# PE operands at one address modulo 256, scores grouped by form, and the u/z stage begun within v's last steps

## The chip, the cores and the metric

The kernel runs on one core of one Trainium2 chip. The metric is the time of one execution on the device in microseconds (us); smaller is better. The core's engines run side by side, each with its own queue of instructions that it works through in order: PE (TensorE, matmuls; its weight loads are listed apart as PEld), DVE (VectorE), ACT (ScalarE), POOL (GpSimd) and SP (SyncE, which here issues DMAs). They wait for one another by semaphores.

## The reference

One gMLP layer, then one sliding-window attention layer, on x of 1024 tokens by 1024 channels, all in float32:

```python
u, v, z = split(rms_norm(x) @ w_in, 3)          # 2048 channels each
u = gelu(u); v = layer_norm(gelu(v))
s = causal(w_s) applied to v in chunks of 128 tokens, per group of 256 channels, + b_s
h = x + rms_norm((u * s * silu(z)) @ w_out)
k, v = rms_norm(h) @ w_k, rms_norm(h) @ w_v     # 4 heads of 64
q, z = split(rms_norm(h) @ b_w_in, 2)           # 16 heads of 64
o = softmax over a window of 128 tokens (with ALiBi and one sink per head) of q k, times v
out = h + rms_norm((o * silu(z)) @ b_w_out)
```

## The kernel before

**Products.** Every large product is computed with float32 operands split into a high part, rounded to the matmul's type fp32r, and a low part, the remainder. `split` (lines 104 to 106) writes both: ACT copies the high part, DVE subtracts for the low one. `mm3` (lines 167 to 170) then issues three matmuls into one PSUM bank, high by high, high by low and low by high, mostly 128x128 weights against 512 columns. `lhsT` is the stationary operand that a weight load puts into the array, `rhs` the moving one.

**Stages.** The program has four, in this order: v (`v_layer`), u and z (`uz_layer`), the first output product (`out_layer`), and the attention layer with its own output product. The products of v, u/z and the first output use a scheme with seven half-size block products instead of eight; they are numbered m = 1 to 7. The sums that the scheme needs of the weights are formed on DVE in v and on POOL in u/z (`f` and `f2` in `prep2`).

**v.** Two passes Q, each over m = 1, 2, 5, 6, 7, 4, 3 with two half steps u: 28 steps. Results gather in PSUM banks `vb` (m = 1, 6, 7, 4) and `vc` (m = 2, 5, 3). ACT and DVE evacuate them into `vslot0`, `vslot1` or `ve6`, ACT applies Gelu, DVE takes statistics, and a DMA stores them as `vd`. At the end DVE and POOL form `ve`, one over the standard deviation. The tiles of this stage lie in the pool `vp`, which closes then.

**u/z.** A pool `up` is opened on the addresses of `vp`, so its tiles may be written only when v's last readers are done. It holds two pairs of split weights (`uzhilo0`, `uzhilo1`), the broadcast row scales `bc`, slots for results (`uz_slots`) and small tiles. For each of 16 column blocks ("quads") `fetch` loads two raw weight tiles of 512 KB (`raw_uz`), `prep1` splits for the products m = 1 and 2, `prep2` forms the sums on POOL and splits for 6 and 5, `prep3` for 7, 3 and 4. The first three calls and `broadcast_rstd` (lines 486 to 494: eight small DVE products with the identity, two matmuls with ones, two copies into `bc`) come before the loop. `group_consts` loads `vg` and `wc` for a group, masks `wc` on POOL and multiplies it by ones into the bank `rb`.

**Attention.** A unit is one block of 128 tokens with four heads; there are 32. `scores` (lines 969 to 976) fills two banks. For each g of two it issues two matmuls with `kh` (128 rows: the high parts of k against q's high and low parts), then two with `kl` (64 rows each, the two halves of the array). Between units the engine works on other products (`qz`, `pk`, `pv`, `ob`), a few at a time.

**What sets the order.** The code is written in the order of dependences; a scheduler then orders each engine's queue, and pools set where tiles lie: one after another, in the order of `big`, `const`, `wpool`, `st`, and then the stage's own pool. Where a tile's address matters, only its residue is spoken of here (bytes within a partition):

| tiles | used as | modulo 512 before | modulo 512 after |
|---|---|---|---|
| `big`: T, n, q, the products' `ohiloP0a`, `ohiloP0b`, `wob` | either operand | 128 | 128 |
| `wpool`: `whi`, `wlo`, with `_g`, `_s`, `_v`; also `uzhilo` | either | 480 | 384 |
| `vp`: `vhi`, `vlo` | moving in v | 224 | 128 |
| `kh`, `kl` | moving in scores | 64 | 384 |

The 512-wide fp32r matmuls are these, by (moving, stationary) residue modulo 512. Before: 408 (128, 128), 2208 (128, 480), 1104 (480, 128), 216 (224, 128). After: 624 (128, 128), 2208 (128, 384), 1104 (384, 128).

Of the kernel before, what the change touches and what calls it, by code (L numbers as in the profile page):

```python
# [14 lines left out]
P = 128  # L15
# [35 lines left out]
def tile_yoco(  # L51
# [36 lines left out]
    ident = const.tile([P, P], F32, name="ident")  # L88
    ones = const.tile([P, P], F32, name="ones")
    nc.vector.memset(ones, 1.0)  # L90
    nhalf = const.tile([P, 4], F32, name="nhalf")
    nc.vector.memset(nhalf, -0.5)
    first = const.tile([P, 1], F32, name="first")
    nc.scalar.activation(first, ones[:, 0:1], AF.Gelu_apprx_tanh)

    def raw_tile(name):
        return wpool.tile([P, 1024], F32, tag="raw", name=f"raw_{name}", bufs=3)
# [109 lines left out]
    def copy(out, a):  # L207
        nc.scalar.activation(out, a, AF.Copy)  # L208
# [30 lines left out]
    def sum_tile(name):  # L239
        return st.tile([P, 1024], F32, tag="xt", name=name)  # L240
# [18 lines left out]
    def x_stats(h, raws):  # L259
# [6 lines left out]
        rstd(rx[h], ss, f"x{h}")  # L266
        yield


    def v_layer():  # L270
        vp_ctx = ExitStack()
        vp = vp_ctx.enter_context(tc.tile_pool(name="vp", bufs=1, reuse_waits="tile"))

        slots = [vp.tile([P, 4, TH], F32, name=f"vslot{i}") for i in range(2)]
        raws = Ring(*[raw_of(wpool, "raw", 3)] * 3, *[raw_of(vp, "vraw", 2)] * 2)
        pieces = Ring(*[pair_of(wpool, "w", 2)] * 2, pair_of(vp, "v", 1))

# [124 lines left out]
        side = chain(x_stats(0, raws), x_stats(1, raws))  # L402

        bank_b = bank_c = None
        a1, e6, e67 = [], None, []
        for n, (Q, m, u) in enumerate(steps):
            if u == 0:
                if m == 1:
                    bank_b = [bank("mm", f"vb{Q}_{t}") for t in range(4)]
                elif m in (2, 5):  # L410
                    bank_c = [bank("s", f"vc{Q}{m}_{t}") for t in range(4)]
            ps = bank_b if m in (1, 6, 7, 4) else bank_c
            first = m in (1, 2, 5)
            hi, lo = ready.pop(n)
            for kk in range(2):
                k = 2 * u + kk
                cs = slice(kk * 512, kk * 512 + 512)
                for t in range(4):
                    ts_ = slice(t * P, (t + 1) * P)
                    mm3(ps[t], T[m][0][:, k, ts_], T[m][1][:, k, ts_], hi[:, cs], lo[:, cs],  # L420
                        first and k == 0, k == HT - 1)
            if n >= 2:
                prep(n + 2)
            if n == 0:
                xload(xa[:, 1], 0, 1, 0, 2)
            elif n == 1:
                prep(3)
                xload(xa[:, 1], 0, 1, 2, 2)
            elif n >= 4:
                step(side)  # L430
            if u == 0:
                continue
            for t in range(4):
                if m == 1:
                    a1.append(slots[0][:, t])
                    copy(a1[t], ps[t])
                elif m == 2:
                    add(a1[t], a1[t], ps[t], ALU.add)
                    if Q:
                        done(a1[t], a1[t], 0, 0, t, Q)  # L440
                elif m == 6:
                    if t == 0:
                        e6 = big.tile([P, 4, TH], F32, tag="P1_3", name=f"ve6_{Q}")
                    copy(e6[:, t], ps[t])
                elif m == 7:
                    e67.append(slots[1][:, t])
                    copy(e67[t], ps[t])
                    add(e67[t], e67[t], bank_c[t], ALU.add)
                    if Q:
# [19 lines left out]


    def uz_layer():
        up_ctx = ExitStack()
        up = up_ctx.enter_context(tc.tile_pool(name="up", bufs=1, reuse_waits="tile"))
        two = [up.tile([P, 2, 1024], F32R, name=f"uzhilo{i}") for i in range(2)]
        w = pair_of(wpool, "w", 2)
        pieces = Ring(w, lambda name: [two[0][:, i] for i in range(2)], w, lambda name: [two[1][:, i] for i in range(2)])
        bc = up.tile([P, NH, TH], F32, name="bc")
        more = up.tile([P, 6, TH], F32, name="uz_slots")
        four = big.tile([P, 4, TH], F32, tag="P1_3", name="uz_slots4")
        slots = [more[:, i] for i in range(6)] + [four[:, i] for i in range(4)]  # L480
        taken = [0]
# [5 lines left out]
        def broadcast_rstd():
            for h in range(NH):
                dg = sum_tile(f"dg{h}")[:, 0:512].rearrange("p (a b) -> p a b", a=4)
                for j in range(4):  # L490
                    nc.vector.tensor_scalar(dg[:, j], ident, rx[h][:, j:j + 1], None, ALU.mult)
                ps = bank("s", f"bc{h}")
                nc.tensor.matmul(ps, lhsT=ones, rhs=dg.rearrange("p a b -> p (a b)"), start=True, stop=True)
                copy(bc[:, h], ps)

        quads = [(g, zz) for g in range(G) for zz in range(2)]
        raws, ops, acc = {}, {}, {}
# [106 lines left out]
            scale(c[0, 0], 0)  # L604

        fetch(0)
        prep1(0)
        prep2(0)
        broadcast_rstd()
        group_consts(0)  # L610
        fetch(1)
        prev = None
# [252 lines left out]
    for _ in range(8):  # L865
        nc.tensor.matmul(warm[:, 0:P], lhsT=ones, rhs=ones, start=True, stop=True)
    nc.scalar.dma_start(out=ident, in_=consts[:, C_ID:C_ID + P])
    v_layer()
    uz_layer()
    n0, yo, ss = out_layer()  # L870


# [4 lines left out]
    nc.sync.dma_start(out=mrg, in_=consts[:, C_MERGE:C_MERGE + P])  # L877
    mprev = bp.tile([P, P], F32, name="mprev")
    nc.sync.dma_start(out=mprev, in_=consts[:, C_PREV:C_PREV + P])
    qsc = bp.tile([P, 2], F32, name="qsc")  # L880
    nc.sync.dma_start(out=qsc, in_=consts[:, C_QS:C_QS + 2])
    neg = bp.tile([P, P], F32, name="neg")
    nc.vector.memset(neg, -1e30)
    snk = bp.tile([P, 4, 4], F32, name="snk")
    nc.sync.dma_start(out=snk.rearrange("p a b -> p (a b)"), in_=sinks.partition_broadcast(P))

    kh = [bp.tile([P, 2, S], F32R, name=f"kh{i}") for i in range(2)]
    kl = bp.tile([P, 2, S], F32R, name="kl")
# [62 lines left out]
    class Unit:  # L951
# [4 lines left out]
        def scores(self):  # L956
# [8 lines left out]
            for par in range(2):  # L965
                pss.append(bank("s", f"s{self.id}_{par}").rearrange("p (g s) -> p g s", g=2))
            ks = slice(b * P - P + w0, (b + 1) * P)
            for g in range(2):
                m = p * 4 + gp * 2 + g
                for par in range(2):  # L970
                    nc.tensor.matmul(pss[par][:, g, w0:256], lhsT=q[par][:, m, bs_], rhs=kh[par][:, p, ks],
                                     start=True, stop=False)
                for par in range(2):
                    rw = half[par]
                    nc.tensor.matmul(pss[par][:, g, w0:256], lhsT=q[par][rw, m, bs_], rhs=kl[rw, p, ks],
                                     start=False, stop=True)
# [96 lines left out]
        return ss  # L1073

    def final(h, t, yo, ss):
        e = const.tile([P, 1], F32, tag="ef", name=f"ef{h}_{t}", bufs=2)
        r = const.tile([P, 1], F32, tag="rf", name=f"rf{h}_{t}", bufs=2)
        nc.vector.tensor_scalar(e, ss[:, 0, t:t + 1], 1.0 / D, EPS, ALU.mult, ALU.add)
        nc.vector.tensor_scalar(r, ss[:, 1, t:t + 1], 1.0 / D, e, ALU.mult, ALU.add)
        nc.gpsimd.tensor_tensor(r, r, nhalf[:, 0:1], ALU.pow)  # L1080
        xt = load_tok(h1d[h][t], f"hf{h}_{t}")
        for i in range(2):
            cs = slice(i * 512, i * 512 + 512)
            nc.vector.scalar_tensor_tensor(yo[:, cs], yo[:, cs], r, xt[:, cs], ALU.mult, ALU.add)
# [116 lines left out]
```

## Time and profile before

| | us |
|---|---|
| times of three runs | 1102.64, 1105.35, 1106.91 |
| their median | 1105.35 |
| the profiled execution | 1105.53 |
| its span in the trace | 1103.6 |
| PE's idle time by what it waited for, the longest | 2.4 (DVE `uzhilo`), 1.6 (DVE `yoa`, twice), 1.3 (DVE `pr`), 1.3 (ACT `uzhilo`) |

The stages in the trace, by the starts of their products: v to about 166 us, u/z from 166.1 to about 518, the first output product from 519 to 681, and the attention layer from there to the end.

The lines below are quoted from several views. A row of the timeline gives the start and the duration in us, the engine, the line in the code, and what is written and read (`out<-in`). [1.27 <-ACT ...] is idle time before it and who ended it. A row of the groups gives the count, the summed busy time in us, the mean of one in ns, and the idle time before them. A row of the windows gives the window, its length, then for PE, PEld, DVE, ACT and POOL the busy time and the count in brackets, then PE's granted clock, the DMA engines' busy share and GB/s.

### The profile page before, as it was taken

The page shows a single profiled execution, that of the slowest core. Times are in us where ns is not written, and L with a number is a line of the kernel's source. Part 1 is how long each engine was busy: PE and PEld are TensorE (multiplying, and loading weights), DVE is VectorE, ACT ScalarE, POOL GpSimd, SP SyncE. Part 2 cuts the span into 40 slices and gives each one's busy share as a digit, 9 for nine tenths or more (in the row PEclk, how much of TensorE's full clock was granted, in tenths as well). Part 3 has the DMA queues.
Part 4 walks back from the last instruction along what each step waited for, and adds up shares of the span by engine and source line. Part 5 has one row for each costly group of instructions (what it writes and reads, how often), then busy time and mean ns, then how long its engine had stood idle before and what let it go on. Part 6 is the DMA issues. An engine that isn't in the chain of part 4 may idle for free.

```text
span 1103.6 us, 14200 instructions
## 1 busy us (share of the span) xinstructions
PE 1084.6 (98%) x5108; PEld 864.7 (78%) x5108; DVE 782.2 (71%) x1335; ACT 583.5 (53%) x983; POOL 284.9 (26%) x199
## 2 busy tenths in 40 slices
PE   9999998999999999999999999999999999999997
PEld 7877886888888888888878878788778767777776
DVE  6987457767767668677695796746768975767773
ACT  6674344565565555454444554536676465665530
POOL 0000023253343441540661211313212322200120
PEclk9999999999999999999999999999999999999999
DMA  8876252234333423348967633724111212112343
GB/s 293 285 274 246 104 163 79 100 105 139 120 115 110 145 99 129 106 137 271 343 239 277 209 115 96 263 96 153 58 58 59 77 58 77 58 58 77 116 172 114
DMA packets 68709, 159.75 MB, mean 145 GB/s; under 512 B 6176, under 2 KB 16800, under 8 KB 68640
## 3 DMA queue, kind: packets, MB, share of 16 engines
q1 hardware_dynamic: 63744, 150.37, 39.9%
q10 hardware_dynamic: 4896, 8.48, 2.1%
q8 instruction: 40, 0.66, 0.3%
q14 instruction: 29, 0.24, 0.1%
HBM read 127.37 MB, written 31.46 MB: 144 GB/s over the span
## 4 chain that ended last, share of the span: by engine, by line
PE 86%; DVE 7%; issue 3%; ACT 1%; POOL 1%; DMA 1%; DVEq 0%; POOLq 0%; ACTq 0%
PE ub L170 5%; PE ub L169 5%; PE ub L168 5%; PE ob L169 5%; PE qz L168 5%; PE ob L168 5%; PE ob L170 5%; PE qz L170 5%; PE qz L169 5%; PE uc L170 3%; PE uc L169 3%; PE uc L168 3%; PE sp L577 3%; PE vb L169 2%; PE vb L170 2%
## 5 line engine op out<-in xcount | busy, mean ns | idle before, releaser
L140 POOL TENSOR_TENSOR raw_w<-raw_w,gn 128x1024 f32<-128x1024 f32 x32 | 66.0, 2063 | 187.0 <-DMA raw_w<-in_wqz_dram 158.2
L168 PE MATMUL qz<-n_hi,whi 128*128 128x512 f32 x256 | 103.6, 405 | 0.1
L170 PE MATMUL qz<-n_hi,wlo 128*128 128x512 f32 x256 | 101.6, 397 | 0.7 <-DVE wlo L106 0.7
L169 PE MATMUL qz<-n_lo,whi 128*128 128x512 f32 x256 | 101.6, 397 | 0.0
L106 DVE TENSOR_TENSOR wlo<-raw_w,whi 128x1024 fp32r<-128x1024 f32 x40 | 55.0, 1375 | 33.5 <-ACT whi L105 33.2
L1008 POOL TENSOR_SCALAR_AFFINE_SELECT pc<-pc 128x512 f32<-128x512 f32 x32 | 25.7, 804 | 162.0 <-ACT pc L1007 150.3
L105 ACT ACTIVATE whi<-raw_w 128x1024 fp32r<-128x1024 f32 x40 | 42.2, 1055 | 37.0 <-PE qz L169 17.6
L170 PEld LDWEIGHTS qz<-n_hi,wlo 128*128 128x128 f32 x256 | 48.2, 188 | 12.6 <-DVE wlo L106 1.1
L168 PEld LDWEIGHTS qz<-n_hi,whi 128*128 128x128 f32 x256 | 48.2, 188 | 12.0 <-ACT pr L991 0.4
L106 DVE TENSOR_TENSOR uzhilo<-f,uzhilo 128x1024 fp32r<-128x1024 f32 x31 | 39.1, 1263 | 25.3 <-ACT uzhilo L105 25.3
L169 PEld LDWEIGHTS qz<-n_lo,whi 128*128 128x128 f32 x256 | 48.3, 189 | 10.6
L205 POOL TENSOR_TENSOR f<-raw_uz,raw_uz 128x512 f32<-128x512 f32 x16 | 21.6, 1348 | 132.7 <-DVE uzhilo L106 132.7
L105 ACT ACTIVATE uzhilo<-f 128x1024 fp32r<-128x1024 f32 x31 | 32.8, 1059 | 42.8 <-PE uc L169 41.0
L991 ACT ACTIVATE pr<-pr,nm 128x129 f32<-128x129 f32 x128 | 49.8, 392 | 7.7 <-DVE nm L989 5.3
L170 PE MATMUL ub<-T,uzhilo 128*128 128x512 f32 x128 | 51.2, 400 | 2.4 <-DVE uzhilo L106 2.4
L168 PE MATMUL ub<-T,uzhilo 128*128 128x512 f32 x128 | 52.3, 409 | 0.0
L168 PE MATMUL ub<-T,whi_g 128*128 128x512 f32 x128 | 51.5, 402 | 0.2 <-ACT whi_g L105 0.2
L208 ACT ACTIVATE uz_slots<-ub 128x512 f32<-128x512 f32 x48 | 28.5, 594 | 42.7 <-PE ub L170 42.7
L168 PE MATMUL uc<-T,uzhilo 128*128 128x512 f32 x124 | 49.8, 401 | 1.3 <-ACT uzhilo L105 1.3
L169 PE MATMUL ub<-T,uzhilo 128*128 128x512 f32 x128 | 51.0, 398 | 0.0
L170 PE MATMUL ub<-T,wlo_g 128*128 128x512 f32 x128 | 50.8, 397 | 0.0
L169 PE MATMUL ub<-T,whi_g 128*128 128x512 f32 x128 | 50.7, 396 | 0.0
(316 smaller groups left out, 3300.6 us busy)
## 6 DMA issues: line engine op xcount, KB each, us to landing
raw_uz<-in_wuz_in_dram SPq DMA_DIRECT2D x32, 512.0 KB, 3.5
raw_w<-in_wqz_dram SPq DMA_DIRECT2D x32, 512.0 KB, 3.5
td<-uz_slots SPq DMA_DIRECT2D x56, 256.0 KB, 2.1
orawP2a<-td SPq DMA_DIRECT2D x28, 512.0 KB, 4.6
raw<-in_wv_in_dram SPq DMA_DIRECT2D x17, 512.0 KB, 5.1
orawP2b<-in_wo_a_dram SPq DMA_DIRECT2D x17, 512.0 KB, 6.7
vg<-vd SPq DMA_DIRECT2D x8, 1024.0 KB, 5.4
raw_o<-in_wo_a_dram SPq DMA_DIRECT2D x15, 512.0 KB, 5.2
```

The source lines that it names most:

```text
L105: nc.scalar.activation(hi, src, AF.Copy)
L106: nc.vector.tensor_tensor(lo, src, hi.bitcast(F32), ALU.subtract)
L140: nc.gpsimd.tensor_tensor(rv, rv, g, ALU.mult)
L168: nc.tensor.matmul(out, lhsT=a_hi, rhs=b_hi, start=start, stop=False, skip_group_check=True)
L169: nc.tensor.matmul(out, lhsT=a_hi, rhs=b_lo, start=False, stop=False, skip_group_check=True)
L170: nc.tensor.matmul(out, lhsT=a_lo, rhs=b_hi, start=False, stop=stop, skip_group_check=True)
L205: (eng or nc.vector).tensor_tensor(out, a, b, op)
L208: nc.scalar.activation(out, a, AF.Copy)
L577: nc.tensor.matmul(psv[:, n], lhsT=d["vg"][:, 4 * j + n, i * P:(i + 1) * P], rhs=d["wc"], start=True, stop=True)
L991: nc.scalar.activation(pr[:, i], pr[:, i], AF.Exp, bias=nm[:, i // 2, i % 2:i % 2 + 1], accum_out=dn[:, i // 2, i % 2:i % 2 + 1])
L1008: nc.gpsimd.affine_select(pc, pc, [[0, 4], [1, P]], ALU.is_ge, 0.0, base=0, channel_multiplier=-1)
```

## The change

There are three parts.

1. Addresses. `first` and `nhalf` become one tile, as do `ef` and `rf`; `bc` moves from `up` to the constant tile of tag `gpost`, which the gain `gpa` used from the start and now takes over when `bc` has had its last use. The pools behind `const` thereby begin 96 bytes earlier modulo 512 (the table above). `qsc` and `snk` move behind `kh` and `kl`.
2. Scores. All four matmuls with `kh` come first, then all four with `kl`; one accumulation group covers the bank.
3. The start of u/z. `uz_layer` becomes a generator of which `v_layer` takes one step in each of its last three steps: `fetch(0)`, `prep1(0)`, `prep2(0)`. The pairs `uzhilo` take over the tags `shared0` and `shared1` of v's slots, tile by tile, in a pool `uv` that stays open over both stages. `broadcast_rstd` runs in v, after m = 2 of the second pass.

```diff
-    nhalf = const.tile([P, 4], F32, name="nhalf")
+    small = const.tile([P, 5], F32, name="small")
+    nhalf = small[:, 0:4]
     nc.vector.memset(nhalf, -0.5)
-    first = const.tile([P, 1], F32, name="first")
-    nc.scalar.activation(first, ones[:, 0:1], AF.Gelu_apprx_tanh)
+    nc.scalar.activation(small[:, 4:5], ones[:, 0:1], AF.Gelu_apprx_tanh)
...
+    bc = const.tile([P, NH, TH], F32, tag="gpost", name="bc")
...
+    uv_ctx = ExitStack()
+    uv = uv_ctx.enter_context(tc.tile_pool(name="uv", bufs=1, reuse_waits="tile"))
+
+    def shared(i, shape, dtype, name):
+        return uv.tile(shape, dtype, tag=f"shared{i}", name=name)
...
-        slots = [vp.tile([P, 4, TH], F32, name=f"vslot{i}") for i in range(2)]
+        slots = [shared(i, [P, 4, TH], F32, f"vslot{i}") for i in range(2)]
...
             if n >= 2:
                 prep(n + 2)
+            if n >= len(steps) - 3:
+                step(ahead)
...
+            if Q == 1 and m == 2:
+                broadcast_rstd()
...
-        two = [up.tile([P, 2, 1024], F32R, name=f"uzhilo{i}") for i in range(2)]
         w = pair_of(wpool, "w", 2)
-        pieces = Ring(w, lambda name: [two[0][:, i] for i in range(2)], w, lambda name: [two[1][:, i] for i in range(2)])
-        bc = up.tile([P, NH, TH], F32, name="bc")
...
+        def half_of(i):
+            def take(name):
+                t = shared(i, [P, 2, 1024], F32R, f"uzhilo{i}_{name}")
+                return [t[:, 0], t[:, 1]]
+
+            return take
+
+        pieces = Ring(w, half_of(0), w, half_of(1))
...
         fetch(0)
+        yield
         prep1(0)
+        yield
         prep2(0)
-        broadcast_rstd()
+        yield
+        up_ctx = ExitStack()
+        up = up_ctx.enter_context(tc.tile_pool(name="up", bufs=1, reuse_waits="tile"))
...
-    v_layer()
-    uz_layer()
+    uz = uz_layer()
+    v_layer(uz)
+    drain(uz)
+    uv_ctx.close()
...
             for g in range(2):
                 m = p * 4 + gp * 2 + g
                 for par in range(2):
                     nc.tensor.matmul(pss[par][:, g, w0:256], lhsT=q[par][:, m, bs_], rhs=kh[par][:, p, ks],
-                                     start=True, stop=False)
+                                     start=g == 0, stop=False, skip_group_check=True)
+            for g in range(2):
+                m = p * 4 + gp * 2 + g
                 for par in range(2):
                     rw = half[par]
                     nc.tensor.matmul(pss[par][:, g, w0:256], lhsT=q[par][rw, m, bs_], rhs=kl[rw, p, ks],
-                                     start=False, stop=True)
+                                     start=False, stop=g == 1, skip_group_check=True)
...
-        e = const.tile([P, 1], F32, tag="ef", name=f"ef{h}_{t}", bufs=2)
-        r = const.tile([P, 1], F32, tag="rf", name=f"rf{h}_{t}", bufs=2)
+        er = const.tile([P, 2], F32, tag="ef", name=f"ef{h}_{t}", bufs=2)
+        e, r = er[:, 0:1], er[:, 1:2]
```

**The order on ACT near the end of v.** Here ACT evacuates the banks `vb` of m = 7 in the second pass into `vslot`; `whi` before them belongs to m = 4. A row has the line, the operation, what is written and read, and its size. Before:

```order
L105 ACTIVATE whi_1088<-raw_12_1086 128x1024
L105 ACTIVATE whi_1118<-raw_13_1116 128x1024
L208 ACTIVATE vslot_117<-vb_0_774 128x512
L208 ACTIVATE vslot_117<-vb_1_775 128x512
L363 ACTIVATE vslot_117<-vslot_117,rx_90 128x512
L208 ACTIVATE vslot_117<-vb_2_776 128x512
```

In the changed kernel the same place reads:

```order
L105 ACTIVATE whi_1107<-raw_12_1105 128x1024
L105 ACTIVATE whi_1137<-raw_13_1135 128x1024
L105 ACTIVATE uzhilo_g_0_1295<-f_1291 128x1024
L208 ACTIVATE vslot_120<-vb_0_777 128x512
L208 ACTIVATE vslot_120<-vb_1_778 128x512
L208 ACTIVATE vslot_120<-vb_2_779 128x512
```

The first split of `uzhilo` has moved from behind v's end to a place ahead of the evacuations.

**The order on PE behind v.** `ub` with `whi_g` is the first product of u/z (m = 1); what follows uses the pair `uzhilo`. Before:

```order
L170 MATMUL ub_1348<-T_122,wlo_g_0_1304 128x512
L168 MATMUL uc_1408<-T_259,uzhilo_1294 128x512
L169 MATMUL uc_1408<-T_259,uzhilo_1294 128x512
L168 MATMUL ub_1348<-T_346,uzhilo_1294 128x512
L169 MATMUL ub_1348<-T_346,uzhilo_1294 128x512
L168 MATMUL ub_1448<-T_122,whi_g_1_1377 128x512
L170 MATMUL ub_1348<-T_346,uzhilo_1294 128x512
L168 MATMUL ub_1348<-T_346,uzhilo_1294 128x512
L169 MATMUL ub_1348<-T_346,uzhilo_1294 128x512
L170 MATMUL ub_1348<-T_346,uzhilo_1294 128x512
L493 MATMUL bc_1320<-dg_1315,ones 128x512
L168 MATMUL ub_1348<-T_346,uzhilo_1294 128x512
```

In the changed kernel, from the same product on:

```order
L170 MATMUL ub_1349<-T_125,wlo_g_0_1264 128x512
L168 MATMUL uc_1410<-T_262,uzhilo_g_0_1295 128x512
L169 MATMUL uc_1410<-T_262,uzhilo_g_0_1295 128x512
L170 MATMUL uc_1410<-T_262,uzhilo_g_0_1295 128x512
L168 MATMUL uc_1410<-T_262,uzhilo_g_0_1295 128x512
```

The products `uc` and `ub` now stand whole, one behind the other, and the two matmuls `bc` are gone from here.

**The order of a score unit on PE.** `s` are the unit's two banks. Before:

```order
L971 MATMUL s_1_1_0_6850<-kh_4938,q_hi 128x256
L971 MATMUL s_1_1_1_6851<-kh_4939,q_lo 128x256
L975 MATMUL s_1_1_0_6850<-kl,q_hi 128x256
L975 MATMUL s_1_1_1_6851<-kl,q_lo 128x256
L971 MATMUL s_1_1_0_6850<-kh_4938,q_hi 128x256
L971 MATMUL s_1_1_1_6851<-kh_4939,q_lo 128x256
L975 MATMUL s_1_1_0_6850<-kl,q_hi 128x256
L975 MATMUL s_1_1_1_6851<-kl,q_lo 128x256
```

In the changed kernel:

```order
L997 MATMUL s_1_1_0_6883<-kh_4967,q_hi 128x256
L997 MATMUL s_1_1_1_6884<-kh_4968,q_lo 128x256
L997 MATMUL s_1_1_0_6883<-kh_4967,q_hi 128x256
L997 MATMUL s_1_1_1_6884<-kh_4968,q_lo 128x256
L1003 MATMUL s_1_1_0_6883<-kl,q_hi 128x256
L1003 MATMUL s_1_1_1_6884<-kl,q_lo 128x256
L1003 MATMUL s_1_1_0_6883<-kl,q_hi 128x256
L1003 MATMUL s_1_1_1_6884<-kl,q_lo 128x256
```

The two pairs with `kl` have moved together to the unit's end.

More of the change, by code (lines that the diff above doesn't have):

```diff
@@ L267, in x_stats, with broadcast_rstd, v_layer @@
         yield
-    def v_layer():
+    bc = const.tile([P, NH, TH], F32, tag="gpost", name="bc")
+    def broadcast_rstd():
+        for h in range(NH):
+            dg = sum_tile(f"dg{h}")[:, 0:512].rearrange("p (a b) -> p a b", a=4)
+            for j in range(4):
+                nc.vector.tensor_scalar(dg[:, j], ident, rx[h][:, j:j + 1], None, ALU.mult)
+            ps = bank("s", f"bc{h}")
+            nc.tensor.matmul(ps, lhsT=ones, rhs=dg.rearrange("p a b -> p (a b)"), start=True, stop=True)
+            copy(bc[:, h], ps)
+    uv_ctx = ExitStack()
+    uv = uv_ctx.enter_context(tc.tile_pool(name="uv", bufs=1, reuse_waits="tile"))
+    def shared(i, shape, dtype, name):
+        return uv.tile(shape, dtype, tag=f"shared{i}", name=name)
+    def v_layer(ahead):
         vp_ctx = ExitStack()
         vp = vp_ctx.enter_context(tc.tile_pool(name="vp", bufs=1, reuse_waits="tile"))
-        slots = [vp.tile([P, 4, TH], F32, name=f"vslot{i}") for i in range(2)]
+        slots = [shared(i, [P, 4, TH], F32, f"vslot{i}") for i in range(2)]
         raws = Ring(*[raw_of(wpool, "raw", 3)] * 3, *[raw_of(vp, "vraw", 2)] * 2)
@@ L404, in v_layer @@
         bank_b = bank_c = None
+        ahead = iter(ahead)
         a1, e6, e67 = [], None, []
@@ L471, in uz_layer @@
     def uz_layer():
-        up_ctx = ExitStack()
-        up = up_ctx.enter_context(tc.tile_pool(name="up", bufs=1, reuse_waits="tile"))
-        two = [up.tile([P, 2, 1024], F32R, name=f"uzhilo{i}") for i in range(2)]
         w = pair_of(wpool, "w", 2)
-        pieces = Ring(w, lambda name: [two[0][:, i] for i in range(2)], w, lambda name: [two[1][:, i] for i in range(2)])
-        bc = up.tile([P, NH, TH], F32, name="bc")
[L478 to L481, printed above, removed]
+        def half_of(i):
[4 more added lines that the diff above has]
+        pieces = Ring(w, half_of(0), w, half_of(1))
+        slots, taken = [], [0]
         def slot():
@@ L485, in slot @@
             return slots[(taken[0] - 1) % len(slots)]
[L487 to L494, printed above, removed]
         quads = [(g, zz) for g in range(G) for zz in range(2)]
@@ L606, in uz_layer @@
         fetch(0)
+        yield
         prep1(0)
+        yield
         prep2(0)
-        broadcast_rstd()
+        yield
+        up_ctx = ExitStack()
+        up = up_ctx.enter_context(tc.tile_pool(name="up", bufs=1, reuse_waits="tile"))
+        more = up.tile([P, 6, TH], F32, name="uz_slots")
+        four = big.tile([P, 4, TH], F32, tag="P1_3", name="uz_slots4")
+        slots += [more[:, i] for i in range(6)] + [four[:, i] for i in range(4)]
         group_consts(0)
@@ L879, in tile_yoco @@
     nc.sync.dma_start(out=mprev, in_=consts[:, C_PREV:C_PREV + P])
+    neg = bp.tile([P, P], F32, name="neg")
+    nc.vector.memset(neg, -1e30)
+    kh = [bp.tile([P, 2, S], F32R, name=f"kh{i}") for i in range(2)]
+    kl = bp.tile([P, 2, S], F32R, name="kl")
     qsc = bp.tile([P, 2], F32, name="qsc")
     nc.sync.dma_start(out=qsc, in_=consts[:, C_QS:C_QS + 2])
-    neg = bp.tile([P, P], F32, name="neg")
-    nc.vector.memset(neg, -1e30)
     snk = bp.tile([P, 4, 4], F32, name="snk")
     nc.sync.dma_start(out=snk.rearrange("p a b -> p (a b)"), in_=sinks.partition_broadcast(P))
-    kh = [bp.tile([P, 2, S], F32R, name=f"kh{i}") for i in range(2)]
-    kl = bp.tile([P, 2, S], F32R, name="kl")
     half = [slice(0, 64), slice(64, P)]
```

## The prediction

> **What bounds the kernel now.** I read the page's head and chain first, then the waits of PE, then PE's timeline, for the spacing of its matmuls.
>
> ```profile
> span 1103.6 us, 14200 instructions
> PE 1084.6 (98%) x5108; PEld 864.7 (78%) x5108; DVE 782.2 (71%) x1335; ACT 583.5 (53%) x983; POOL 284.9 (26%) x199
> PE 86%; DVE 7%; issue 3%; ACT 1%; POOL 1%; DMA 1%; DVEq 0%; POOLq 0%; ACTq 0%
> ```
>
> PE is busy 98% of the span and is 86% of the chain that ends last. So PE bounds nearly every stage, and the time can fall in two ways only: the matmuls start closer together, or PE waits less. The ends of matmuls are modelled, so I use starts alone.
>
> **Part 1, the addresses.** How many matmuls change, and by how much? The first row counts all matmuls of line 168, the first of the three passes of every product; the others are groups that are to be taken off.
>
> ```profile
> 0.00:1103.60 1103.60, 543.66 (x1376) 259.54 (x1376) 1.00 0.42 145
> L168 PE MATMUL pv<-whi,n_hi 128*128 128x256 f32 x64 | 18.1, 282 | 0.1
> L168 PE MATMUL ob<-wob_hi,q_hi 128*128 128x512 f32 x64 | 25.2, 394 | 0.0
> L168 PE MATMUL ob<-ohiloP0b,ohiloP0a 128*128 128x512 f32 x40 | 15.7, 391 | 0.0
> L168 PE MATMUL oc<-ohiloP0b,ohiloP0a 128*128 128x512 f32 x32 | 12.6, 394 | 0.0
> ```
>
> 1376 - 64 = 1312 of them are 512 wide, 3936 in the three passes. The last three groups take both operands from `big`: they already have equal residues, 3 x (64 + 40 + 32) = 408 matmuls. The other 3528 pair a tile of `big` with one of another pool, 96 bytes off. The out stage runs both kinds one after the other, in the same loop and with nothing waited for:
>
> ```profile
> 577.81 0.39 PE L168 MATMUL ob<-ohiloP0b,ohiloP0a 128*128 128x512 f32 x1
> ...
> 580.98 0.39 PE L170 MATMUL ob<-ohiloP0b,ohiloP0a 128*128 128x512 f32 x1
> 581.21 0.40 PE L168 MATMUL ob<-whi_s,ohiloP0b 128*128 128x512 f32 x1
> ...
> 586.59 0.40 PE L170 MATMUL ob<-whi_s,ohiloP0b 128*128 128x512 f32 x1
> ```
>
> The equal pairs take (580.98 - 577.81) / 14 = 226.4 ns from start to start, the unequal ones (586.59 - 581.21) / 23 = 233.9 ns: 7.5 ns apart. Two more stretches give the bounds: the u/z stage (unequal, 13 gaps) and the last stage just after PE had been interrupted (equal, 22 gaps).
>
> ```profile
> 299.79 0.39 PE L169 MATMUL ub<-T,whi_g 128*128 128x512 f32 x1
> ...
> 302.84 0.40 PE L170 MATMUL ub<-T,wlo_g 128*128 128x512 f32 x1
> 1050.01 0.39 PE L169 MATMUL ob<-wob_lo,q_hi 128*128 128x512 f32 x1
> ...
> 1055.03 0.39 PE L170 MATMUL ob<-wob_hi,q_lo 128*128 128x512 f32 x1
> ```
>
> They give 234.6 and 228.2 ns. The saving per matmul lies between 233.9 - 228.2 = 5.7 and 234.6 - 226.4 = 8.2 ns, if the residues are the cause: 20 to 29 us for 3528; and it is nothing if they are not. I take 6.5 ns, because other matmuls interrupt the stream in the attention and u/z stages, where the 228.2 is the nearer row: **-22.9 us**. The 256-wide matmuls become equal too; no row shows one with equal residues, so they get nothing, and the bound is half the 512-wide saving on 416 of them, 1.4 us, with the same loss on the other side.
>
> [...]
>
> **Part 2, the scores.** One unit in the trace, up to the next instruction of PE:
>
> ```profile
> 949.52 0.28 PE L971 MATMUL s<-kh,q_hi 128*128 128x256 f32 x1
> 949.63 0.28 PE L971 MATMUL s<-kh,q_lo 128*128 128x256 f32 x1
> 949.84 0.38 PE L975 MATMUL s<-kl,q_hi 64*128 64x256 f32 x1
> ...
> 950.15 0.38 PE L971 MATMUL s<-kh,q_hi 128*128 128x256 f32 x1
> 950.37 0.28 PE L971 MATMUL s<-kh,q_lo 128*128 128x256 f32 x1
> 950.58 0.38 PE L975 MATMUL s<-kl,q_hi 64*128 64x256 f32 x1
> ...
> 950.89 0.66 PE L1022 MATMUL o<-pc,vt 128*64 128x256 f32 x4
> L971 PE MATMUL s<-kh,q_hi x64: 222/318/387, 766.0 to 1047.5; 128*128 128x256 f32 x56, 128*128 128x128 f32 x8
> ```
>
> The gaps: 0.11 from full to full matmul, 0.21 from full to the half-height pair (both of its members start together), 0.31 from the pair to what follows, and 0.22 in the second half, where full follows full just behind a pair. A unit is 1.37 us. Grouped by form it is full x4 (three gaps of 0.11), 0.21 to the first pair, X to the second, 0.31 to what follows: 0.85 + X. No row shows pair behind pair. X is at least 0.11, the full to full gap, and at most 0.31, the pair to full gap. I take 0.21, what a pair takes behind a full one, since a pair's own weights are what differs there: 1.06, a saving of 0.31. 56 / 2 = 28 units of this width, and 8 / 2 = 4 of half width, at which I put the same: 32 x 0.31 = **-9.9 us**, between 6.7 (X = 0.31) and 13.1 (X = 0.11).
>
> **Part 3, the start of u/z.**
>
> ```profile
> 168.67 0.39 PE L170 MATMUL ub<-T,wlo_g 128*128 128x512 f32 x1
> 170.33 0.50 PE L168 MATMUL uc<-T,uzhilo 128*128 128x512 f32 x1 [1.27 <-ACT uzhilo L105]
> ...
> 174.71 0.80 PE L170 MATMUL ub<-T,uzhilo 128*128 128x512 f32 x1 [2.44 <-DVE uzhilo L106]
> ...
> 176.58 1.74 PE L493 MATMUL bc<-dg,ones 128*128 128x512 f32 x2
> 177.50 1.05 PE L168 MATMUL ub<-T,uzhilo 128*128 128x512 f32 x1
> ...
> 180.71 0.40 PE L169 MATMUL ua<-T,whi_g 128*128 128x512 f32 x1
> ```
>
> PE waits twice for the pair `uzhilo`, which lies where v's slots lay and so is written only when v's pool closes; behind the longer wait it runs slower for a while (0.59 us to the next start). From 168.67 to 180.71 are 12.0 us with 16 gaps between 512-wide products (16 x 0.234 = 3.7), two pairs of `bc` (2 x 0.92 = 1.8, as 176.58 to 177.50) and a small `rb`: 6.3 us are lost. In the changed kernel the pair is written during v, so both waits go. `bc` costs its 1.8 us in v instead; its eight small DVE instructions lie beside PE's work there. What is late next is `rb`, behind the load of `wc` and the GpSimd pass over it, which follows `ve`: it comes within about half a microsecond of PE, so I leave 0.4 of the loss: -5.9 us.
>
> Against it stands a **new wait**. In the changed order ACT does the first `uzhilo` split ahead of the four evacuations of m = 7 into `vslot`; it waits there for the third GpSimd sum of `f`, and the evacuations are queued behind it. PE's first product of m = 4 needs the first one's bank.
>
> ```profile
> 141.79 1.30 ACT L208 ACTIVATE vslot<-vb 128x512 f32<-128x512 f32 x2 [2.44 <-PE vb L170]
> 142.47 1.29 POOL L205 TENSOR_TENSOR f<-f,raw_uz 128x512 f32<-128x512 f32 x1
> 143.69 0.40 PE L168 MATMUL vb<-whi,T 128*128 128x512 f32 x1
> L105 ACT ACTIVATE uzhilo<-f 128x1024 fp32r<-128x1024 f32 x31 | 32.8, 1059 | 42.8 <-PE uc L169 41.0
> ```
>
> The sum ends at 142.47 + 1.29 = 143.76, the split at 144.82, the first evacuation at about 145.5, while PE wants the bank at 143.69: +1.8 us. The whole stream shifts with it, so the later evacuations and the split's other half on DVE cost at most a few tenths. It is nothing if the load comes 2 us earlier, and up to 2.7 if PE runs slow behind it as it does at 174.71. Part 3 together: -5.9 + 1.8 = **-4.1**, between -6 and -2.
>
> **What keeps the gain from reaching the end.** A faster PE meets the engines that were just in time.
>
> ```profile
> 525.00:550.00 25.00, 25.00 (x109) 20.29 (x109) 17.08 (x9) 12.21 (x14) 15.92 (x7) 1.00 0.99 350
> 544.00:575.00 31.00, 31.00 (x135) 24.98 (x134) 31.00 (x18) 12.17 (x18) 26.41 (x8) 1.00 0.75 269
> PE ob L169 <- DVE ohiloP0b L106: 0.6, 1, 0.6
> 850.00:905.00 55.00, 53.27 (x269) 39.63 (x267) 49.72 (x124) 32.49 (x83) 17.28 (x14) 1.00 0.18 58
> ```
>
> From 544 to 575 DVE is busy all 31 us, and PE waits for it at the end (0.6): of the 135 x 6.5 ns = 0.9 us that PE would gain there, I give all back. From 850 to 905 DVE is busy 49.72 of 55 and PE idles 1.7 already; at most 269 x 6.5 ns = 1.7 us and the share of a few score units would be won there, some 3 us, and I give back half, 1.5. `gpa` now takes the place of `bc`, so its load moves from the start into the stretch whose DMA share is 0.99; four loads of 512 KB are issued ahead of the operands there as before, and nothing wants it until about 570, so nothing is added. Together **+2.5**, between 1 and 6.
>
> **The sum.** -22.9 - 9.9 - 4.1 + 2.5 = -34.4 from the profiled execution, 1105.5 (span 1103.6 and 1.9 around it; the median of the runs is 1105.35, within 0.2): **1071 us**.
>
> **The rivals.**
> 1. *The residue that counts is one modulo 512.* All tiles of `big` are at 128 modulo 512, so the 408 fast matmuls are equal by that measure too, and the trace before can't tell the two. After the change the other pools are at 384: only 216 products of v (`vhi`, `vlo`) become equal modulo 512, which saves 1.4 us. The sum is -1.4 - 9.9 - 4.1 + 1 = -14.4, **1091 us**. That the fast pairs come from one pool speaks for it; that the whole 512 is needed is shown by nothing. That the addresses have no part in it at all (the slow tiles share other properties, such as being rewritten all the time) ends at the same place: 1092. [...]
> 2. *Half a period apart is worse than 96 bytes apart.* The same modulus of 512, with a conflict that grows with the distance: 3312 products then lie exactly 256 apart. If that costs another 6.5 ns each, it is -1.4 + 21.5 - 9.9 - 4.1 = +6.1, **1112 us**, slower. The point from which it decides is 4.2 ns a product. The two distances in the trace (96 one way for `whi_s`, 96 the other for `whi_g`) take 233.9 and 234.6, with no growth to be seen, so this is unlikely.
> 3. *The reserve was thin.* DVE eats more: in the u/z and attention stages it is at 60 to 90% beside a PE that gets 3% faster. With +6 for the stretches, X at 0.31 and 2.7 us at the new wait the sum is -22.9 - 6.7 - 3 + 6 = -26.6: **1079 us**.
> 4. *The grouping saves less*, because a pair behind a pair waits as long as a full matmul behind a pair: X = 0.31, and the sum is 3.2 us higher, **1074 us**, inside the forecast's own range. The trace has 0.22 for full behind full in the unit's second half, which speaks for less. [...]
>
> **How the numbers follow.** Forecast (1065 to 1077) 0.62, of which rival 4 has 0.2; rival 3 (1077 to 1086) 0.18; rival 1, in both its forms, 0.15; rival 2 0.05. The 8 in 10 need the forecast, rival 3 and, for the bounds of the alignment term (29 instead of 23 us, at the low end), a reach down to 1064; upwards I go to 1088, short of rival 1. Faster by over 0.5% (5.5 us, about what a measurement of this kernel can tell from no change) is 0.93, within it 0.02, slower 0.05.
>
> **What would show it.** Part 1: starts of `qz`, `ub` and `vc<-whi` 227 to 228 ns apart; if they stay at 234 while `vb<-vhi` falls to 227, it is rival 1, at 240 for the rest it is rival 2. Part 2: a unit of 1.06 us, X readable between the two `kl` pairs. Part 3: no wait for `uzhilo` behind the first `ub`, `bc` in v's second half, and one new wait of about 1.8 us on ACT at the first product of m = 4. The last term: waits for DVE near 575 and from 850 to 905. The forecast is wrong by most if the spacing does not move.

## The result, and the profile after

The changed kernel takes **1074.54 us** (median of 4 runs, 1073.83 to 1077.21) against 1104.99 before (median of 4): a ratio of 0.973, 95% interval 0.9704 to 0.9755. The forecast was 1071, faster; the range 1064 to 1088 holds the result. The profiled execution is the slowest of the four, 1077.21 us with a span of 1075.5; what it has beyond the others is taken up in the last section.

The page's head and chain after the change:

```profile
span 1075.5 us, 14187 instructions
PE 1051.4 (98%) x5108; PEld 859.1 (80%) x5108; DVE 781.6 (73%) x1335; ACT 582.7 (54%) x983; POOL 282.3 (26%) x199
PE 79%; DVE 11%; ACT 3%; issue 2%; DMA 2%; POOL 2%; DVEq 0%; POOLq 0%; ACTq 0%
```

PE's busy time fell by 33 us, the span by 28: some of the gain came back as idle time. DVE's share of the chain rose from 7 to 11%, ACT's from 1 to 3%. The same two stretches of PE's timeline that carried part 1 (first and last row of 13 gaps in u/z and of 23 in the out stage; the same instructions in the same places):

```profile
289.25 0.39 PE L169 MATMUL ub<-T,whi_g 128*128 128x512 f32 x1
...
292.20 0.39 PE L170 MATMUL ub<-T,wlo_g 128*128 128x512 f32 x1
565.48 0.39 PE L170 MATMUL ob<-whi_s,ohiloP0b 128*128 128x512 f32 x1
...
570.70 0.39 PE L169 MATMUL ob<-wlo_s,ohiloP0a 128*128 128x512 f32 x1
```

That is 2.95 / 13 = 226.9 and 5.22 / 23 = 227.0 ns, where they were 234.6 and 233.9. One score unit, up to PE's next instruction:

```profile
927.48 0.28 PE L997 MATMUL s<-kh,q_hi 128*128 128x256 f32 x1
927.59 0.28 PE L997 MATMUL s<-kh,q_lo 128*128 128x256 f32 x1
927.71 0.28 PE L997 MATMUL s<-kh,q_hi 128*128 128x256 f32 x1
927.83 0.28 PE L997 MATMUL s<-kh,q_lo 128*128 128x256 f32 x1
928.04 0.38 PE L1003 MATMUL s<-kl,q_hi 64*128 64x256 f32 x1
...
928.26 0.28 PE L1003 MATMUL s<-kl,q_hi 64*128 64x256 f32 x1
...
928.47 0.66 PE L1050 MATMUL o<-pc,vt 128*64 128x256 f32 x4
```

It takes 0.99 us instead of 1.37. X, which no row had shown, is 0.22, and the second pair is followed after 0.21, not 0.31. The border from m = 7 to m = 4 near v's end, on PE, POOL and ACT:

```profile
142.38 0.39 PE L170 MATMUL vb<-vhi,T 128*128 128x512 f32 x1
144.62 0.50 PE L168 MATMUL vb<-whi,T 128*128 128x512 f32 x1 [1.85 <-ACT vslot L208]
141.70 1.29 POOL L205 TENSOR_TENSOR f<-f,raw_uz 128x512 f32<-128x512 f32 x1
143.02 1.06 ACT L105 ACTIVATE uzhilo_g<-f 128x1024 fp32r<-128x1024 f32 x1 [4.59 <-POOL f L205]
143.98 0.58 ACT L208 ACTIVATE vslot<-vb 128x512 f32<-128x512 f32 x1
```

ACT idles 4.59 us in front of the split until POOL's third sum ends, with the evacuations queued behind it, and PE waits 1.85 us: the forecast had 1.8. The waits for `uzhilo` behind v are gone. The longest waits of PE:

```profile
PE pt L1032 <- DVE pr L1026: 3.2, 3, 1.9
PE oc L168 <- DVE yoa L205: 2.4, 2, 1.9
PE o L1053 <- DVE pp L1039: 2.0, 2, 1.7
PE vb L168 <- ACT vslot L208: 1.8, 1, 1.8
PE ob L169 <- DVE ohiloP0b L106: 1.6, 1, 1.6
PE qz L170 <- DVE wlo L106: 1.2, 1, 1.2
```

The five for DVE come to 10.4 us; before they were 1.3 + 1.6 + 0 + 0.6 + 0.7 = 4.2.

### The profile page after: what moved, and what is told of

Its sections match the earlier page's. It is cut to its first block, busy times and chain, and to the rows that moved or that the text cites. A ratio compares the mean times of both kernels' runs of the same rounds, so it can differ in the third digit from the quotient of the medians.

```text
span 1075.5 us, 14187 instructions
## 1 busy us (share of the span) xinstructions
PE 1051.4 (98%) x5108; PEld 859.1 (80%) x5108; DVE 781.6 (73%) x1335; ACT 582.7 (54%) x983; POOL 282.3 (26%) x199
## 4 chain that ended last, share of the span: by engine, by line
PE 79%; DVE 11%; ACT 3%; issue 2%; DMA 2%; POOL 2%; DVEq 0%; POOLq 0%; ACTq 0%
PE ub L168 5%; PE ub L170 5%; PE ub L169 5%; PE ob L168 5%; PE ob L169 5%; PE ob L170 5%; PE qz L168 4%; PE qz L170 4%; PE qz L169 4%; PE uc L168 3%; PE uc L170 3%; PE uc L169 3%; PE sp L592 3%; PE vb L168 2%; PE vb L169 2%
## 5 line engine op out<-in xcount | busy, mean ns | idle before, releaser
L106 DVE TENSOR_TENSOR wlo<-raw_w,whi 128x1024 fp32r<-128x1024 f32 x40 | 57.7, 1443 | 32.0 <-ACT whi L105 28.7
L105 ACT ACTIVATE whi<-raw_w 128x1024 fp32r<-128x1024 f32 x40 | 42.2, 1055 | 34.6 <-PE qz L169 15.4
L105 ACT ACTIVATE uzhilo_g<-f 128x1024 fp32r<-128x1024 f32 x31 | 32.9, 1060 | 50.0 <-PE uc L170 42.6
L106 DVE TENSOR_TENSOR uzhilo_g<-f,uzhilo_g 128x1024 fp32r<-128x1024 f32 x31 | 39.0, 1257 | 21.9 <-ACT uzhilo_g L105 21.9
L205 POOL TENSOR_TENSOR f<-raw_uz 128x512 f32<-128x512 f32 x16 | 20.6, 1291 | 126.6 <-DMA raw_uz<-in_wuz_in_dram 71.7
L168 PE MATMUL ub<-T,uzhilo_g 128*128 128x512 f32 x128 | 50.5, 394 | 0.0
L170 PE MATMUL ub<-T,uzhilo_g 128*128 128x512 f32 x128 | 49.9, 390 | 0.0
L169 PE MATMUL ub<-T,uzhilo_g 128*128 128x512 f32 x128 | 49.8, 389 | 0.0
```

What stands on the lines that cost most here:

```text
L105: nc.scalar.activation(hi, src, AF.Copy)
L106: nc.vector.tensor_tensor(lo, src, hi.bitcast(F32), ALU.subtract)
L168: nc.tensor.matmul(out, lhsT=a_hi, rhs=b_hi, start=start, stop=False, skip_group_check=True)
L169: nc.tensor.matmul(out, lhsT=a_hi, rhs=b_lo, start=False, stop=False, skip_group_check=True)
L170: nc.tensor.matmul(out, lhsT=a_lo, rhs=b_hi, start=False, stop=stop, skip_group_check=True)
L205: (eng or nc.vector).tensor_tensor(out, a, b, op)
```

## The experiments

The theory was the prediction's: three gains that add up, each on PE, less waits for DVE that a faster PE meets. Its rivals were that the addresses have no part in it, or count modulo 512, or only through the alignment of each operand, that DVE swallows the scores' gain, and that the waits left over come from loads. Times are medians; before is 1104.6 to 1105.8 in all of the comparisons.

### Each part alone, or taken out

**Part 1 alone**, in the kernel before:

```diff
-    nhalf = const.tile([P, 4], F32, name="nhalf")
+    small = const.tile([P, 5], F32, name="small")
+    nhalf = small[:, 0:4]
...
+    kh = [bp.tile([P, 2, S], F32R, name=f"kh{i}") for i in range(2)]
+    kl = bp.tile([P, 2, S], F32R, name="kl")
     qsc = bp.tile([P, 2], F32, name="qsc")
...
-        e = const.tile([P, 1], F32, tag="ef", name=f"ef{h}_{t}", bufs=2)
-        r = const.tile([P, 1], F32, tag="rf", name=f"rf{h}_{t}", bufs=2)
+        er = const.tile([P, 2], F32, tag="ef", name=f"ef{h}_{t}", bufs=2)
...
```

`bc` stays in `up` here; its move goes with part 3.

> The kernel before with part 1 of the change alone (all pools behind the constants 96 bytes lower; scores and start of u/z as before). If the equal residues modulo 256 make the matmuls faster: 3528 matmuls at 227.3 instead of about 233.8 ns, -23 us of PE, less the waits for DVE that a faster PE meets (about 5 us of the 8 seen in the changed kernel), so 1085 to 1088 us. If the addresses have no part in it: 1105, and spacing 234.

Measured: 1087.12 us, ratio 0.9844 (0.9822 to 0.9865), so -17.8 us. In its trace the mean spacing of all uninterrupted 512-wide matmuls is 227.4 ns. Its profiled execution is 19.1 us shorter than that of the kernel before (spans of 1084.5 and 1103.6): the regular gaps lose 22.4 us, and 3.3 come back, most of it in waits:

```profile
PE oc L168 <- DVE yoa L205: 2.3, 2, 1.8
PE pt L1004 <- DVE pr L998: 1.6, 2, 1.4
PE ob L169 <- DVE ohiloP0b L106: 1.6, 1, 1.6
PE qz L170 <- DVE wlo L106: 1.3, 1, 1.3
```

`yoa`, `ohiloP0b` and `wlo` have already grown to what they are in the changed kernel; `pr` has hardly moved.

**Part 1 taken out** of the changed kernel, by 96 bytes and nothing else:

```diff
-    small = const.tile([P, 5], F32, name="small")
+    small = const.tile([P, 29], F32, name="small")
```

> The changed kernel with the tile small 96 bytes longer, so that all pools behind the constants lie at 480 modulo 512 as before, and nothing else changes. If the residues are the cause: spacing of the pairs with big back at 233 to 235 ns, +21 us on PE less some 5 us of waits for DVE that go again: 1090 to 1094. If the order of work was the cause: 1074.5.

Measured: 1092.35 us, ratio 0.9881 (0.9854 to 0.9908): +17.8 us on the changed kernel, the same size from the other side. No instruction differs, and the order on every engine is the same in the two traces; only addresses differ, so the order of work has no part in this. Here `ohiloP0b` is back at 0.5, while `pr` stays at 3.0: that wait belongs to the grouped scores, not to the addresses.

**Part 2 taken out** of the changed kernel:

```diff
                 for par in range(2):
                     nc.tensor.matmul(pss[par][:, g, w0:256], lhsT=q[par][:, m, bs_], rhs=kh[par][:, p, ks],
-                                     start=g == 0, stop=False, skip_group_check=True)
-            for g in range(2):
-                m = p * 4 + gp * 2 + g
+                                     start=True, stop=False)
...
-                                     start=False, stop=g == 1, skip_group_check=True)
+                                     start=False, stop=True)
```

> The changed kernel with the eight score matmuls of a unit in the order of before. PE's gaps in the 32 units grow by 11.6 us (56 to 44 us summed in the two traces). If all of it reaches the end: 1086. If the attention stage is held by DVE for part of it, the waits there (pt for pr, o for pp: some 5 us more in the changed kernel than before) shrink again: 1081 to 1084. If grouping is worth nothing because DVE sets the pace: 1074 to 1076.

Measured: 1083.77 us, ratio 0.9814 (0.9791 to 0.9837): +9.2 of the 11.6 us that the gaps of the units grow by (31.8 us for the 32 units in the changed kernel, 43.5 here, 43.4 before). So 80% of the scores' gain reaches the end, and PE's waits for DVE take most of the rest: `pr` is 1.5 us here and 3.2 in the changed kernel, `pp` 1.5 and 2.0.

**Part 3 taken out**: `v_layer` and `uz_layer` are those of before, the rest is the changed kernel.

```diff
-    uz = uz_layer()
-    v_layer(uz)
-    drain(uz)
-    uv_ctx.close()
+    v_layer()
+    uz_layer()
```

> The changed kernel without part 3: addresses and grouped scores are kept, the u/z stage opens its pool after v again and bc is broadcast there. By the prediction's own sums part 3 is worth 6.3 us of waits removed less 1.9 us for the new wait: +4 us, 1078 to 1079, with the waits for uzhilo back (1.3 and 2.4 us) and none on ACT vslot. Rival: the start of u/z was hidden elsewhere and the time stays within 1 us of the changed kernel's 1074.5.

Measured: 1079.08 us, ratio 0.9765 (0.9747 to 0.9783): +4.5 us. The two waits are back as they were before the change:

```profile
PE ub L170 <- DVE uzhilo L106: 2.4, 1, 2.4
PE uc L168 <- ACT uzhilo L105: 1.4, 1, 1.4
```

The three, 17.8 + 9.2 + 4.5 = 31.5, come to the whole of 30.5 within the scatter of the runs.

**The new wait.** One index moves the last evacuation of v into the other slot, so that the pair that takes over that slot can't be split early:

```diff
-                    c = slots[Q][:, t]
+                    c = slots[0][:, t]
```

> The changed kernel with one index changed: m = 4 of the second pass evacuates into vslot0 instead of vslot1, so the first uzhilo split, which takes over vslot0's slot, can't be placed ahead of the evacuations of m = 7. If that placement makes the new 1.85 us wait of PE for ACT vslot, it goes, and nothing else moves: 1072 to 1073.5. If something else held those evacuations (the banks, DVE): 1074.5 with the wait still there; if the splits now come too late for the uc product: a wait for uzhilo and 1075 or more.

Measured: 1071.10 us, ratio 0.9698 (0.9678 to 0.9719). The wait for ACT `vslot` is gone, and no wait for `uzhilo` has come in its place. Its interval and the changed kernel's overlap slightly (0.9704 to 0.9755), so the gain of some 3 us is likely, not certain. It is more than the expectation's 1.5 to 2.5; 1.85 us of it are seen in the trace, where the same place now reads, without a gap:

```profile
140.49 0.39 PE L170 MATMUL vb<-vhi,T 128*128 128x512 f32 x1
140.72 0.39 PE L168 MATMUL vb<-whi,T 128*128 128x512 f32 x1
```

### Which distance counts

The next four are the changed kernel with other distances between the two operands, set by the length of `small` ([P, 13], [P, 21], [P, 37]) or, for the last, by a tile of 96 bytes ahead of all pools.

> The changed kernel with the tile small 32 bytes longer: operands 32 bytes apart modulo 256. If any inequality modulo 256 costs the same: spacing 234, 1090 to 1094. If only a distance from 64 bytes on costs: 227 and 1074.5. If 64-byte alignment of each operand is what counts: slow too.

> The changed kernel with the tile small 64 bytes longer: operands 64 bytes apart modulo 256, both multiples of 64. If equality modulo 256 counts: 234 ns, 1090 to 1094. If alignment to 64 bytes counts: 227 ns and 1074.5.

> The changed kernel with the tile small 128 bytes longer: operands 128 bytes apart modulo 256, both multiples of 128. If equality modulo 256 counts: 234 ns, 1090 to 1094. If equality modulo 128, or alignment to 128 bytes, is enough: 227 ns and 1074.5. If the cost grows with the distance: over 236 ns.

> The changed kernel with a tile of 96 bytes ahead of everything, so that both operands lie at 224 modulo 256: equal, but no multiple of 64 or 128. If equality of the two counts: 227 ns and 1074 to 1077. If each operand's own alignment (to 64 or 128 bytes) counts: 233 ns and 1090 or more.

The spacing in the two stretches, worked out as above from first and last row, and the time:

| distance modulo 256 | `ub`, moving operand in `big` | `ob`, moving operand in the other pool | us |
|---|---|---|---|
| 0, both at 128 (changed kernel; 256 apart) | 226.9 | 227.0 | 1074.54 |
| 0, both at 224 (256 apart) | 227.7 | 226.5 | 1075.55, one run |
| 32 | 233.8 | 233.0 | 1094.04, one run |
| 64 | 233.8 | 228.7 | 1090.74, one run |
| 96 | 234.6 | 233.5 | 1092.35 |
| 128 | 232.3 | 233.0 | 1085.92, one run |

Rows behind three of them, 13 gaps each at 64 and at 224, then 23 at 64:

```profile
292.92 0.40 PE L169 MATMUL ub<-T,whi_g 128*128 128x512 f32 x1
...
295.96 0.39 PE L170 MATMUL ub<-T,wlo_g 128*128 128x512 f32 x1
```

```profile
287.83 0.39 PE L172 MATMUL ub<-T,whi_g 128*128 128x512 f32 x1
...
290.79 0.39 PE L173 MATMUL ub<-T,wlo_g 128*128 128x512 f32 x1
```

```profile
574.74 0.39 PE L170 MATMUL ob<-whi_s,ohiloP0b 128*128 128x512 f32 x1
...
580.00 0.39 PE L169 MATMUL ob<-wlo_s,ohiloP0a 128*128 128x512 f32 x1
```

The figures of the two columns are good to some 0.8 ns, as starts are given to 0.01 us. In these runs equality is what counts, not the alignment of either operand: 224 is a multiple of 32 only and is fast (227.7 and 226.5), 64 and 128 apart are multiples of 64 and 128 and are slow (233.8 and 232.3 in `ub`). Equality modulo 128 is not enough (128 apart: 232.3 and 233.0), modulo 512 is not needed (256 apart is fast: 226.9 and 227.0). The cost in `ub` doesn't grow with the distance: 233.8, 233.8, 234.6 and 232.3 at 32, 64, 96 and 128. At 128 the time is 4 us below the expected 1090 to 1094: the mean of all uninterrupted 512-wide gaps is 232.1 ns there, 233.3 at 96, and its granted clock is 1.00 from 850 to 895 us and 0.998 over the whole span (the last section has what some others lose there). That 64 bytes cost little in one direction (228.7) and all in the other (233.8) was in no theory, and is left open. It is no accident of one stretch: in the same trace `vb` and `vc` with `whi` from the later pool as the moving operand are 229 ns apart on average, `ub` and `qz` with the moving operand from `big` 233.

### Where the gain was lost

**GpSimd's sums in the out stage.** On top of the version with the one index, GpSimd's sums are moved to DVE: all twelve, then only the four of m = 7.

```diff
-                add(s, s, r, ALU.subtract, nc.gpsimd)
+                add(s, s, r, ALU.subtract)
...
-                add(d, r, s, ALU.subtract, nc.gpsimd)
+                add(d, r, s, ALU.subtract)
...
-                add(s_view(u), s_view(u), a22, ALU.add, nc.gpsimd)
+                add(s_view(u), s_view(u), a22, ALU.add)
```

> The kernel of slot0_for_m4 with the twelve GpSimd sums of the first output product moved to DVE. If DVE is late near 557 us because its instructions take 3.4 instead of 1.2 us beside GpSimd's sums: DVE's take 1.2 there, PE's wait for ohiloP0b (1.6) goes, the wait for yoa stays: 1069 to 1070. If DVE in its order now waits for the loads of those sums (DMA is 0.99 busy there): new waits of PE on DVE in 510 to 560, 1072 to 1078. If the wait for ohiloP0b comes from the load of orawP2a: 1071, unchanged.

> As out_adds_on_dve, but only the four sums of m = 7 (into tmp) move to DVE. GpSimd's sums of m = 6 (530 to 544 us) still slow DVE, those at 544 to 550 no longer do. Under the first theory the wait for ohiloP0b shrinks from 1.6 to under 0.8: 1070 to 1070.5. Under the load theory: unchanged, 1071.

Measured: 1068.43 us, ratio 0.9657 (0.9632 to 0.9681), and 1068.62, ratio 0.9673 (0.9646 to 0.9700). The wait for `ohiloP0b` is gone in both; that of `yoa` stays, at 2.5 and 2.6. Both times are below what was expected, and both intervals touch that of the kernel they start from (0.9678 to 0.9719), so their gain of some 2.5 us is likely, not certain. The same instructions of DVE in the changed kernel, with GpSimd's sums beside them, and with all sums on DVE:

```profile
542.50 3.41 DVE L106 TENSOR_TENSOR ohiloP0a<-orawP2a,ohiloP0a 128x1024 fp32r<-128x1024 f32 x1
545.83 3.41 DVE L106 TENSOR_TENSOR wlo_s<-scho,whi_s 128x1024 fp32r<-128x1024 f32 x1
541.44 6.72 POOL L205 TENSOR_TENSOR scho<-scho,raw_o 128x1024 f32<-128x1024 f32 x2
```

```profile
538.87 1.23 DVE L106 TENSOR_TENSOR ohiloP0a<-orawP2a,ohiloP0a 128x1024 fp32r<-128x1024 f32 x1
540.01 1.22 DVE L106 TENSOR_TENSOR wlo_s<-scho,whi_s 128x1024 fp32r<-128x1024 f32 x1
```

Each of these two takes 3.41 us beside GpSimd's sums and 1.22 or 1.23 without them: DVE has more to do and is done sooner. The load theories fall, as no new wait of PE on DVE came and `ohiloP0b` is no longer late. What holds DVE up beside GpSimd is not shown.

**The late `pr` in attention.** In the version with all sums on DVE, a 128x4 instruction of DVE, whose median is 0.16 us, takes 1.75 us beside GpSimd's product of a weight tile with the gain:

```profile
854.05 1.90 POOL L140 TENSOR_TENSOR raw_w<-raw_w,gn 128x1024 f32<-128x1024 f32 x1 [2.69 <-DVE mx L1013]
```

```profile
854.22 1.75 DVE L1017 TENSOR_SCALAR nm<-mx 128x4 f32<-128x4 f32 x1
```

So it was moved to ACT:

```diff
-            nc.vector.tensor_scalar(nm, mx, -1.0, None, ALU.mult)
+            nc.scalar.activation(nm, mx, AF.Copy, scale=-1.0)
```

> The kernel of out_adds_on_dve with the small instruction nm (minus the row maximum, 128x4) moved from DVE to ACT. In its trace nm takes 0.16 us at best and 1.75 us where GpSimd's 1.90 us product of the weights with the gain runs beside it (854.22 to 855.97 beside 854.05 to 855.95), and PE then waits 1.9 us for pr. If the late pr comes from nm being held up there: PE's waits for pr and pp (3.3 and 2.1) shrink below 2 together, no phase of PE at half speed behind them, 1064 to 1067. If the next DVE instruction is held up just as long and pr stays late: 1068 to 1070. If ACT's queue makes nm later still: 1070 or more.

Measured: 1074.86 us, ratio 0.9732 (0.9705 to 0.9758): slower by 6 us than the kernel it was made from, a miss. PE's wait for `pr` shrank from 3.3 to 0.5, but that for `pp`, next in DVE's order, grew from 2.1 to 3.8, and that for GpSimd's `pc` from 0.2 to 1.0. One of DVE's multiplications, 0.69 us at 849.46 in the same trace, takes 1.90 us beside GpSimd's product:

```profile
813.04 1.90 POOL L140 TENSOR_TENSOR raw_w<-raw_w,gn 128x1024 f32<-128x1024 f32 x1 [3.32 <-DMA raw_w<-in_wqz_dram]
813.59 1.90 DVE L1026 TENSOR_TENSOR pr<-pr,dn 128x512 f32<-128x512 f32 x1
```

With `nm` on DVE two of these were held up, for 1.45 and 1.83 us, so the move did not bring this about. `pr` no longer stays late, as the second theory has it; the time lies in the range of the third, and DVE's waits for ACT's `pr` grew from 22.4 to 36.3 us, which speaks for ACT's queue. But the edit also changed the order of PE's queue, in 77 of 5108 places, so the run doesn't show which it is. Nor is the size settled: the three waits of PE sum to 0.3 us less than before, and the two profiled executions are 2.4 us apart, not 6.

## Why the prediction was right, and where its sizes were off

- **Part 1, the addresses: right.** 6.5 ns were taken for 3528 matmuls, -22.9 us; the mean of the uninterrupted gaps is 227.4 in the changed kernel, where the unequal pairs had 233.9 before, and the regular gaps lose 22.4 in the kernel with part 1 alone. The rival that only equality modulo 512 counts falls with the first row of the table, and with it the one that half a period apart is worse (which, with the 1.4 us of the 216 products in its sum, decides from 15.4 / 3312 = 4.6 ns on, not 4.2). The operands' addresses alone are worth 17.8 us here.
- **Part 2, the scores: mechanism right, size too small.** -9.9 was forecast, the gaps lose 11.6. X was right (0.22 for 0.21). The term that was off is the last one: what follows the second pair was left at 0.31, and it is 0.21. In the kernel with the old order and the new addresses the unit is 1.385 us, as before, so the order alone does this; why the first pair shortens what follows the second is not shown. Rival 4 falls: X is 0.22, not 0.31. That the measured time is close to this rival's 1074 is a coincidence.
- **Part 3: right.** -5.9 + 1.8 = -4.1 was forecast; 4.5 measured by taking it out, with the new wait at 1.85 where it was placed. `bc` costs what it did (1.71 us from 107.95 to 109.66 before the next product, 1.84 before). The first gaps behind `bc` and behind the new wait are 0.34 and 0.33 us instead of 0.23. Part of what is saved is clock: without part 3 the granted clock is 0.50 from 169.6 to 176.2, behind the two waits for `uzhilo`.
- **The reserve: too thin.** +2.5 was forecast, between 1 and 6. In the profiled execution, which took 2.7 us more than the median, the waits for DVE grew by 6.2 us, and 1.6 more went in a phase at a granted clock of 0.51 (below). By the medians 17.8 of the 22.9 us of part 1 and 9.2 of the 11.6 of part 2 reach the end: 7.5 are lost. Of the waits, `ohiloP0b` and the 850 to 905 stretch were named; that `yoa` and `wlo` would grow (+0.8 and +0.5) was not, and the second half of the attention's wait, `pp`, neither.
- **The sum.** The misses, some 2 us of more gain (1.7 in the scores, 0.4 in part 3) and some 5 of more loss (7.5 for 2.5), offset each other in part and leave the forecast 3.5 us low; that it is no more is in part luck. The result is between the forecast and the third rival, which is the mechanism that was under-sized.

## What to carry to other kernels

Compare medians first: two profiled executions of like kernels differ here by 1.9 us through their start alone, and 1.6 us went in a phase at half clock in one of them (next section). Before reordering anything, group the matmuls' start-to-start times by the addresses of both operands: in this kernel one equal residue modulo 256 for the moving and the stationary tile was worth 1.6%, for the length of a few small tiles. When PE gets 3% faster, list the engines that were just in time and expect what was won beside them to come back, and look at instructions of DVE that take three times their best time (3.41 for 1.22 us here) before counting its load. A split that waits for a slow producer should stand behind the evacuations in ACT's queue, or take over a slot that comes free later.

## What was not expected of the hardware

- **Phases at half clock behind some waits of PE, and none behind others as long.** In the changed kernel's profiled execution PE waits 1.89 us for `pr` at 861, and from 863.9 on the starts are 0.43 us apart for some 3.4 us; the granted clock from 863.9 to 867.3 is 0.51, in the window of 10 us below it is 0.83. In the version with one index changed the wait at the same place is 1.84, and the clock stays at 1.00:

```profile
860.00:870.00 10.00, 8.11 (x35) 6.20 (x35) 8.17 (x25) 6.53 (x21) 0.80 (x2) 0.83 0.10 28
```

```profile
856.00:866.00 10.00, 8.16 (x47) 6.35 (x48) 8.10 (x25) 7.63 (x23) 0.72 (x2) 1.00 0.11 31
```

  Of the changed kernel and its variants, four profiled executions show it behind this wait (the changed kernel, the old scores, both versions of the out stage; waits of 1.5 to 1.9, granted clocks of 0.76 to 0.90 in the two windows of 5 us around its end), five do not (the version with one index, without part 3, 96 and 128 apart, both at 224; waits of 1.7 to 1.9, a granted clock of 1.00). Some 18 us later PE waits for `pp`: 1.5 to 1.8 us in the four, under 0.5 in the five. With the 1.6 us of the phase that makes some 3 us, and the four are each the slowest of their kernel's runs, by 2.4 to 3.4 us. So most of the `pp` wait above seems to belong to this one execution; that the phase causes it is not shown, only that the two come together. The version with `nm` on ACT shows a phase too (granted clock 0.67 from 850 to 855), and its profiled execution is not its slowest. Behind v's new wait of 1.85 us in the changed kernel the granted clock stays at 1.00 (142.4 to 150.0 us).

  Why waits as long as these end with such a phase in one execution and without it in another is not shown.
- **The start differs from one execution to the next.** Two matmuls of v's first product in the changed kernel and the same two in the version with one index changed:

```profile
8.33 0.63 PE L169 MATMUL vb<-wlo_v,T 128*128 128x512 f32 x1
8.76 0.63 PE L170 MATMUL vb<-whi_v,T 128*128 128x512 f32 x1
```

```profile
7.10 0.40 PE L169 MATMUL vb<-wlo_v,T 128*128 128x512 f32 x1
7.34 0.39 PE L170 MATMUL vb<-whi_v,T 128*128 128x512 f32 x1
```

  In the first trace the starts stay 0.43 us apart until 10.5 us, with the granted clock at 1.00 from 5.6 on, in the second they are 0.23 apart from 5.9 us on. Both start v at 5.60 us, and its 31st matmul starts at 14.9 and at 13.0 us. So 1.9 us between these two traces come from the start, which the edit does not touch.
- **The direction matters at 64 bytes**, in the one run at that distance: 228.7 ns in `ob`, when the moving operand is the one from the later pool, 233.8 in `ub`, when it is the stationary one.
